# Modulation weights fetched one step ahead of their sums, and the last gate vector moved to the last stage's second product

## The chip, the cores and the metric

One Trainium2 chip, one of its NeuronCores. The metric is the device time of one execution in microseconds (us); each kernel has a median over several runs and one profiled execution, whose trace is what is read below. In the rows PE is TensorE (PEld its weight loads), DVE is VectorE, ACT is ScalarE, POOL is GpSimd and SP is SyncE, which here only issues DMAs. A "q" behind the name means the engine's sequencer.

## The reference, cut to what matters

A residual stream x of 512 rows by 1024 columns passes four stages: differential attention, a gated feed-forward product (FFN 1), a token mixer and a second feed-forward product (FFN 2), then a final norm. Stages two to four are modulated by a vector c of 1024 numbers:

```python
mod = (jax.nn.silu(c) @ ada_w[l] + ada_b[l]).reshape(B, N_SUBLAYERS, 3, D_MODEL)
shift, scale, gate = mod[:, :, 0], mod[:, :, 1], mod[:, :, 2]
...
h = modulate(rms_norm_2(x, norm_g[l, 2]), shift[:, 2], scale[:, 2])
x = x + 0.5 * gate[:, 2, None, :] * swiglu(h, ffn2_w_in[l], ffn2_w_out[l])
```

So there are nine modulation vectors of 1024, named (s, kind) below: stage s = 0, 1, 2 for FFN 1, mixer and FFN 2, kind = 0 shift, 1 scale, 2 gate. Each needs a 1024 x 1024 block of `ada_w`, 4 MB, to be read once. The gate (2, 2) is needed only when the second product of FFN 2 is added to x.

## The kernel before

Every large product is done in three TensorE passes: a float32 operand is split into a rounded high part and the rest (`split`, L105: ACT makes the high part, DVE the low part), and high x high, high x low and low x high are summed in PSUM. Weights come by the SP queue into three rotating `raw` buffers (L110) and are split into `whi` and `wlo`, four buffers each. Nearly all other SBUF tiles, the modulation's among them, are taken from one pool of 61 slots of 128 x 512 (`tile`, L102).

**Order.** TensorE's instructions run in the order in which the program emits them. Side work is put into that order by a clock of the program's own: each matmul adds its estimated time to `self.now` (L85), and `later(delay, fn)` (L67) queues a function that is called when the clock passes its due time. `run_until` (L76) calls queued functions early, moving the clock to their due times, until a condition holds. DVE, ACT, POOL and SP get their orders from a scheduler that places what is emitted by priority; each of these queues then runs in order.

**One modulation vector** (`ada`, L446) is made in two halves of 512 columns. For each half, eight steps `one(k, half, acc)` (L463) are queued `step` apart. Step k starts a 256 KB DMA of 128 rows of `ada_w` into a tile `araw` (L466) and right behind it emits the DVE instruction that multiplies it by one column of silu(c) and adds it to `acc` (L469 for k = 0, L471 for the others). After step 7 the sum is split (`ahi`, `alo`), and 21.24 program us later (`DL["ada"]`) `go` (L490) has TensorE sum it over the 128 rows: two products with a tile of ones, 512 columns each, whose result DVE adds to the bias and stores as the half of the vector (L494 to L499). Only one vector is in work at a time (`ada_next`, L504). With `scratch` the tiles lie in the buffers of `hT`, the transposed normed input, which are free between the two products of an FFN, and the fetches go by POOL's DMA queue with four places in rotation; without it they lie in the pool of slots and the fetches go by SP's queue, between the weights' own.

**Where the vectors are made.** (0, 0) and (0, 1) in attention with a step of 6 program us, (0, 2) late in attention with 3; (1, 0) and (1, 1) at the start of the second product of FFN 1, with `scratch`, 2.5; (1, 2), (2, 0) and (2, 1) one after the other in the mixer, 2.5; (2, 2) at the start of FFN 2, 3.0 (L895). `ada_wait` (L509) runs queued work until a vector is complete; `next_norm` (L941) calls it when the first row tile of a stage is finished.

**An FFN** (`ffn`, L874). The first product makes the hidden activations by column blocks of 256: the first block plainly (`gemm_quad`), the other ten by a seven-product Strassen scheme (`fast_feat`, L239), whose sums of weight quarters `S` (L232) and of results `u`, `d` (L266) are DVE's and POOL's work. The second product (`gemm_tok`, L137) splits the activations (`gs`) as it reaches them and multiplies them with `ffn_w_out`, in two halves of 512 columns, each 264 matmuls for four row tiles. When a row tile of a half is summed, `gated_add` (L410) multiplies it by the gate (L427), adds it to x and squares it for the next norm. FFN 1 and FFN 2 run the same code on the same shapes.

Of the kernel before, what the change touches and what calls it, by code (L numbers as in the profile page):

```python
# [18 lines left out]
D = 1024  # L19
KD = D // P  # L20
# [21 lines left out]
class Net:  # L42
# [367 lines left out]
    def gated_add(self, gate, squares, then=None):  # L410

        nc = self.nc

        def evict(half, t, bank):
            if half and then:
                with self.tc.high_priority(offset=PRIO):
                    finish(half, t, bank)
                    then(t)
            else:
                finish(half, t, bank)  # L420

        def finish(half, t, bank):
            if gate is None:
                nc.vector.tensor_tensor(self.x[t][half], bank, self.x[t][half], op=ALU.add)
            else:
                tmp = self.tile("tmp")
                nc.vector.tensor_tensor(tmp, bank, gate[half], op=ALU.mult)  # L427
                nc.vector.tensor_tensor(self.x[t][half], self.x[t][half], tmp, op=ALU.add)
            if squares:
                self.norm_half(t, half)  # L430

        return evict
# [13 lines left out]
    def ada(self, s, kind, step, scratch=False):  # L446


        nc, a = self.nc, self.a
        dst = self.mod[s, kind] = [None, None]  # L450
        if scratch:
            if self.scratch is None:
                self.scratch = [self.hp.tile([P, KD, S], dt, tag=f"hT{i}", name=f"ada{i}") for i, dt in ((0, F32), (1, F32R))]
                self.turn = {}
            sc = self.scratch

        def tile_(name, dt=F32, places=None):
            if not scratch:
                return self.tile(name, dt)
            n = self.turn[name] = self.turn.get(name, -1) + 1  # L460
            return sc[0 if dt == F32 else 1][:, places[n % len(places)], :]

        def one(k, half, acc):  # L463
            c0 = s * 3 * D + kind * D + half * 512
            raw = tile_("araw", places=(0, 1, 6, 7))
            (nc.gpsimd if scratch else nc.sync).dma_start(raw, a["ada_w_2"][0, k * P:(k + 1) * P, c0:c0 + 512])  # L466
            if k == 0:
                acc = tile_("aacc", places=(2, 3))
                nc.vector.tensor_scalar(acc, raw, self.silu_c[:, 0:1], None, op0=ALU.mult)  # L469
            else:  # L470
                nc.vector.scalar_tensor_tensor(acc, raw, self.silu_c[:, k:k + 1], acc, op0=ALU.mult, op1=ALU.add)  # L471
            if k < KD - 1:
                self.later(step, lambda: one(k + 1, half, acc))
                return
            ab = self.tile("ab")
            self.bcast(ab, a["ada_b_2"][0, c0:c0 + 512])
            gb = None
            if kind == 1:
                gb = tile_("gb", places=(4, 5))
                self.bcast(gb, a["norm_g_2"][0, s, half * 512:half * 512 + 512])  # L480
            hi, lo = tile_("ahi", F32R, (0, 1)), tile_("alo", F32R, (2, 3))
            self.split(hi, lo, acc)
            self.later(DL["ada"], lambda: go(half, hi, lo, ab, gb))
            if half == 0:
                self.later(step, lambda: one(0, 1, None))
            else:
                self.ada_busy = False
                self.later(step, self.ada_next)

        def go(half, hi, lo, ab, gb):  # L490
            b = self.bank("sc")
            self.mm(b, self.ones, hi, True, False)
            self.mm(b, self.ones, lo, False, True)
            nc.vector.tensor_tensor(ab, b, ab, op=ALU.add)  # L494
            if kind == 1:
                nc.vector.scalar_tensor_tensor(ab, ab, 1.0, gb, op0=ALU.add, op1=ALU.mult)
            if kind == 2 and s != 1:
                nc.vector.tensor_scalar(ab, ab, 0.5, None, op0=ALU.mult)
            dst[half] = ab  # L499

        self.ada_queue.append(lambda: one(0, 0, None))
        self.ada_next()

    def ada_next(self):  # L504
# [369 lines left out]
    def ffn(self, s, win, wout, nxt):  # L874
        nc = self.nc
        sg, gT, gs = {}, {}, {}

        def gate(i):
            def done(bank, d0, d1):
                for o, d in ((d0[:, :256], bank), (d1, d1), (d0[:, 256:], d0[:, 256:])):  # L880
                    nc.scalar.activation(o, d, AF.Silu)
                sg[i] = d0, d1
            return done

        def up(i):
            def done(bank, *d):
                c = slice(0, 256), slice(256, 512)
                nc.vector.tensor_tensor(d[0][:, c[0]], bank, sg[i][0][:, c[0]], op=ALU.mult)
                nc.gpsimd.tensor_tensor(d[1], d[1], sg[i][1], op=ALU.mult)
                nc.gpsimd.tensor_tensor(d[0][:, c[1]], d[0][:, c[1]], sg[i][0][:, c[1]], op=ALU.mult)  # L890
                for n in range(2):
                    gT[2 * i + n] = d[n]
            return done

        if s == 2:  # L895
            self.ada(2, 2, 3.0)
        wts = [self.load_w(win[g * 512:(g + 1) * 512, c0:c0 + 256], 4, 256) for c0 in (0, FFN) for g in range(2)]
        sta = lambda n: lambda k: tuple(x[:, k % 4, n % 2 * P:n % 2 * P + P] for x in wts[n // 2 * 2 + k // 4])
        first = [self.tile("d0") for _ in range(2)]
        sg[0] = first  # L900

        def ev_up(n, bank):
            gT[n] = sg[0][n]
            nc.vector.tensor_tensor(gT[n], bank, gT[n], op=ALU.mult)

        self.gemm_quad([sta(n) for n in range(4)],
                       [lambda b, n=n: nc.scalar.activation(first[n], b, AF.Silu) for n in range(2)] +
                       [lambda b, n=n: ev_up(n, b) for n in range(2)])
        def split_g(k):
            if k not in gs:  # L910
                gs[k] = self.tile("gs", F32R), self.tile("gs", F32R)
                self.split(*gs[k], gT[k])

        def act(k, t):
            split_g(k)
            return tuple(g[:, t * P:(t + 1) * P] for g in gs[k])

        self.fast_feat([(win[:, c0 + i * 256:c0 + i * 256 + 256], fn(i))
                        for i in range(1, FFN // 256) for c0, fn in ((0, gate), (FFN, up))],
                       lambda: [split_g(k) for k in range(DL["gs"])])  # L920
        if s == 0:
            self.ada(1, 0, 2.5, True)
            self.ada(1, 1, 2.5, True)

        self.ada_wait((s, 2))
        self.norm_reset()
        for half in range(2):
            ev = self.gated_add(self.mod[s, 2], True, self.lazily(nxt) if half else None)
            self.gemm_tok(act, KF, wout[:, half * 512:half * 512 + 512], lambda t, b: ev(half, t, b), 4 if half else 0)
# [512 lines left out]
```

## Time and profile before

| | |
|---|---|
| median of 3 runs | 1874.91 us (1872.62 to 1875.62) |
| the profiled execution | 1875.19 us, span of its instructions 1873.4 us |
| mean granted TensorE clock | 0.992 of full speed |
| busy: PE, PEld, DVE, ACT, POOL | 97%, 86%, 75%, 50%, 21% of the span |
| first product of FFN 1, of FFN 2 | from 597.80 to 831.24 us, from 1501.41 to 1742.55 us |
| fetches of `ada_w` | 112 by SP into `araw`, 32 by POOL into the scratch |

Times in rows are us from the start of the span. An idle time in a row stands in brackets with what ended it; a wait for several things is put down to the last of them.

### The profile page before, as it was taken

The page shows a single profiled execution, that of the slowest core. Times are in us where ns is not written, and L with a number is a line of the kernel's source. Part 1 is how long each engine was busy: PE and PEld are TensorE (multiplying, and loading weights), DVE is VectorE, ACT ScalarE, POOL GpSimd, SP SyncE. Part 2 cuts the span into 40 slices and gives each one's busy share as a digit, 9 for nine tenths or more (in the row PEclk, how much of TensorE's full clock was granted, in tenths as well). Part 3 has the DMA queues.
Part 4 walks back from the last instruction along what each step waited for, and adds up shares of the span by engine and source line. Part 5 has one row for each costly group of instructions (what it writes and reads, how often), then busy time and mean ns, then how long its engine had stood idle before and what let it go on. Part 6 is the DMA issues. An engine that isn't in the chain of part 4 may idle for free.

```text
span 1873.4 us, 29092 instructions
## 1 busy us (share of the span) xinstructions
PE 1820.4 (97%) x10799; PEld 1604.3 (86%) x10799; DVE 1407.5 (75%) x2904; ACT 932.4 (50%) x1696; POOL 400.2 (21%) x380
## 2 busy tenths in 40 slices
PE   8999999999999999999999999999999998999997
PEld 5888777788888999998898778888888898999886
DVE  5568677776966899998365788777868799999633
ACT  5577575465653454553235745664433344554521
POOL 3213114042012122332030211212110022232001
PEclk9999999999999999999999999999999999999999
DMA  4535533625422233357324322222347343333431
GB/s 165 140 113 147 146 107 116 205 67 147 138 92 75 69 106 110 102 173 255 106 69 119 85 57 63 63 62 77 108 157 234 113 135 125 113 102 102 124 113 56
DMA packets 187618, 217.93 MB, mean 116 GB/s; under 512 B 9618, under 2 KB 129826, under 8 KB 187476
## 3 DMA queue, kind: packets, MB, share of 16 engines
q1 hardware_dynamic: 181168, 196.88, 34.9%
q0 software_dynamic: 5584, 18.08, 3.1%
q8 instruction: 85, 1.39, 0.3%
q10 hardware_dynamic: 724, 1.12, 0.2%
q14 instruction: 57, 0.47, 0.1%
HBM read 201.34 MB, written 2.11 MB: 109 GB/s over the span
## 4 chain that ended last, share of the span: by engine, by line
PE 80%; DVE 10%; issue 4%; ACT 2%; POOL 2%; DMA 2%; SPq 0%; POOLq 0%; DVEq 0%; ACTq 0%
PE acc L84 69%; PE sc L84 5%; DVE wlo L107 2%; PE av L84 2%; PE sc L95 1%; DMA araw<-in_ada_w_dram 1%; DVE cvy L1039 1%; PE tr L95 1%; PE tr L785 1%; DVE S L232 1%; PE tr L84 1%; POOL rs L305 1%; ACT whi L106 1%; DMA raw<-in_ffn_w_out_dram 0%; POOL rqk L1094 0%
## 5 line engine op out<-in xcount | busy, mean ns | idle before, releaser
L84 PE MATMUL acc<-hT,whi 128*128 128x256 f32 (+1 forms) x2704 | 642.5, 331 | 5.3 <-DVE d L266 4.8
L84 PEld LDWEIGHTS acc<-hT,whi 128*128 128x128 f32 x2704 | 447.4, 192 | 38.8 <-DVE d L266 5.2
L107 DVE TENSOR_TENSOR wlo<-raw,whi 128x1024 fp32r<-128x1024 f32 (+1 forms) x325 | 331.1, 1028 | 164.3 <-ACT whi L106 162.1
L84 PE MATMUL acc<-hT,wlo 128*128 128x256 f32 (+1 forms) x1352 | 441.2, 326 | 2.9 <-DVE wlo L107 2.8
L106 ACT CAST whi<-raw 128x1024 fp32r<-128x1024 f32 (+1 forms) x325 | 285.5, 880 | 309.9 <-PE acc L84 249.0
L84 PEld LDWEIGHTS acc<-hT,wlo 128*128 128x128 f32 x1352 | 258.5, 191 | 26.1 <-DVE wlo L107 4.1
L84 PE MATMUL acc<-whi,hT 128*128 128x512 f32 x768 | 266.6, 404 | 1.9 <-DVE o L802 0.7
L84 PE MATMUL acc<-whi,gs 128*128 128x512 f32 x704 | 219.1, 390 | 1.8 <-DVE gs L107 1.8
L305 POOL TENSOR_TENSOR rs<-ms,mhalf 128x8 f32<-128x8 f32 (+2 forms) x60 | 86.3, 1439 | 448.9 <-DVE ms L303 360.5
L84 PE MATMUL acc<-T,whi 128*128 128x256 f32 x960 | 174.5, 283 | 0.0
L84 PEld LDWEIGHTS acc<-whi,hT 128*128 128x128 f32 x768 | 144.5, 189 | 32.1 <-DVE hT L107 2.3
L106 ACT CAST whi<-S 128x512 fp32r<-128x512 f32 x160 | 99.4, 621 | 118.7 <-DVE S L232 90.5
L84 PEld LDWEIGHTS acc<-whi,gs 128*128 128x128 f32 x704 | 132.0, 188 | 29.9 <-DVE gs L107 2.6
L84 PE MATMUL acc<-wlo,hT 128*128 128x512 f32 x384 | 150.9, 393 | 3.0 <-DVE wlo L574 3.0
L84 PEld LDWEIGHTS acc<-T,whi 128*128 128x128 f32 x960 | 149.7, 192 | 0.0
L107 DVE TENSOR_TENSOR wlo<-S,whi 128x512 fp32r<-128x512 f32 x160 | 138.6, 885 | 0.5 <-ACT whi L106 0.2
L84 PE MATMUL acc<-wlo,gs 128*128 128x512 f32 x352 | 137.0, 389 | 0.0
L84 PE MATMUL acc<-T,wlo 128*128 128x256 f32 x480 | 135.8, 283 | 0.0
L232 POOL TENSOR_TENSOR S<-raw,S 128x512 f32<-128x512 f32 x40 | 66.8, 1670 | 204.4 <-DVE S L232 196.0
L770 ACT ACTIVATE p<-p,mn 128x128 f32<-128x128 f32 (+3 forms) x128 | 71.1, 556 | 47.4 <-DVE mn L766 45.7
L84 PEld LDWEIGHTS acc<-T,wlo 128*128 128x128 f32 x480 | 92.2, 192 | 0.0
L471 DVE SCALAR_TENSOR_TENSOR aacc<-araw,silu_c,aacc 128x512 f32<-128x512 f32 x98 | 78.9, 805 | 14.0 <-DMA araw<-in_ada_w_dram 13.2
(299 smaller groups left out, 3106.1 us busy)
## 6 DMA issues: line engine op xcount, KB each, us to landing
raw<-in_ffn_w_in_dram SPq DMA_DIRECT2D x88, 512.0 KB, 3.6
raw<-in_l_w_in_dram SPq DMA_DIRECT2D x60, 512.0 KB, 4.1
araw<-in_ada_w_dram SPq DMA_DIRECT2D x112, 256.0 KB, 4.6
raw<-in_mix_w_in_dram SPq DMA_DIRECT2D x53, 512.0 KB, 3.8
raw<-in_ffn_w_out_dram SPq DMA_DIRECT2D x44, 512.0 KB, 3.8
raw<-in_l_w_out_dram SPq DMA_DIRECT2D x16, 512.0 KB, 3.7
ada<-in_ada_w_dram POOLq DMA_DIRECT2D x32, 256.0 KB, 4.2
ab<-in_ada_b_dram POOLq DMA_DIRECT2D x18, 256.0 KB, 4.0
```

The source lines that it names most:

```text
L84: self.nc.tensor.matmul(out, a, b, start=start, stop=stop, skip_group_check=onto)
L95: self.nc.tensor.transpose(out[:, j * P:(j + 1) * P], src(j), self.ident)
L106: return (self.nc.scalar.copy(hi, src), self.nc.vector.tensor_tensor(lo, src, hi.bitcast(F32), op=ALU.subtract))
L107: self.nc.vector.tensor_tensor(lo, src, hi.bitcast(F32), op=ALU.subtract))
L232: sub = lambda o, x, y, op=ALU.subtract, e=nc.vector: e.tensor_tensor(o, x, y, op=op)
L305: pin(nc.gpsimd.tensor_tensor(r[:, :n], ms[:, :n], self.mhalf[:, :n], op=ALU.pow))
L471: nc.vector.scalar_tensor_tensor(acc, raw, self.silu_c[:, k:k + 1], acc, op0=ALU.mult, op1=ALU.add)
L770: nc.scalar.activation(p_[m][:, :L], p_[m][:, :L], AF.Exp, bias=mn[:, m:m + 1], scale=-1.0, accum_out=st[:, m, b:b + 1])
L785: nc.tensor.transpose(tr[:, c * P:(c + 1) * P], p0[:, c * P:(c + 1) * P], self.ident)
L1039: nc.vector.scalar_tensor_tensor(y[:, j:], r[:, :S - j], cw[:, 3 - j, n:n + 1], y[:, j:], op0=ALU.mult, op1=ALU.add)
```

## The change

Three edits. (1) The fetch of step k + 1 is started in step k, ahead of step k's sum, and handed on; the first fetch of a vector is started by `begin`, and its first sum follows one `step` later. (2) The gate vector (2, 2) is no longer queued at the start of FFN 2 with a step of 3.0, by SP and in the pool of slots, but between the two products of FFN 2 with a step of 1.5, by POOL's queue and in the buffers of `hT`. (3) The wait for the gate ahead of the second product stays for FFN 1 only; in its place `finish` runs queued work until the half of the gate that it multiplies by is there.

```diff
@@ -420,6 +420,7 @@
         def finish(half, t, bank):
+            self.run_until(lambda: gate is None or gate[half] is not None)
             if gate is None:
@@ -460,17 +461,22 @@
-        def one(k, half, acc):
+        def fetch(k, half):
             c0 = s * 3 * D + kind * D + half * 512
             raw = tile_("araw", places=(0, 1, 6, 7))
             (nc.gpsimd if scratch else nc.sync).dma_start(raw, a["ada_w_2"][0, k * P:(k + 1) * P, c0:c0 + 512])
+            return raw
+
+        def one(k, half, acc, raw):
+            c0 = s * 3 * D + kind * D + half * 512
+            nxt = fetch((k + 1) % KD, half + (k + 1) // KD) if k < KD - 1 or half == 0 else None
             if k == 0:
                 acc = tile_("aacc", places=(2, 3))
                 nc.vector.tensor_scalar(acc, raw, self.silu_c[:, 0:1], None, op0=ALU.mult)
             else:
                 nc.vector.scalar_tensor_tensor(acc, raw, self.silu_c[:, k:k + 1], acc, op0=ALU.mult, op1=ALU.add)
             if k < KD - 1:
-                self.later(step, lambda: one(k + 1, half, acc))
+                self.later(step, lambda: one(k + 1, half, acc, nxt))
                 return
@@ -482,7 +488,7 @@
             if half == 0:
-                self.later(step, lambda: one(0, 1, None))
+                self.later(step, lambda: one(0, 1, None, nxt))
             else:
@@ -498,7 +504,11 @@
-        self.ada_queue.append(lambda: one(0, 0, None))
+        def begin():
+            raw = fetch(0, 0)
+            self.later(step, lambda: one(0, 0, None, raw))
+
+        self.ada_queue.append(begin)
         self.ada_next()
@@ -892,8 +902,6 @@
-        if s == 2:
-            self.ada(2, 2, 3.0)
         wts = [self.load_w(win[g * 512:(g + 1) * 512, c0:c0 + 256], 4, 256) for c0 in (0, FFN) for g in range(2)]
@@ -921,8 +929,9 @@
         if s == 0:
             self.ada(1, 0, 2.5, True)
             self.ada(1, 1, 2.5, True)
-
-        self.ada_wait((s, 2))
+            self.ada_wait((s, 2))
+        else:
+            self.ada(2, 2, 1.5, True)
         self.norm_reset()
```

## Rows read from the trace of the kernel before

**Rows 1.** The page: busy time and share of the span of each engine.

```profile
PE 1820.4 (97%) x10799; PEld 1604.3 (86%) x10799; DVE 1407.5 (75%) x2904; ACT 932.4 (50%) x1696; POOL 400.2 (21%) x380
```

**Rows 2.** Busy time by stretch: length, PE, PEld, DVE, ACT, POOL; clock, DMA share, GB/s.

```profile
597.80:831.24 233.44, 231.07 (x1921) 230.00 (x1920) 214.55 (x327) 114.70 (x219) 64.68 (x43) 1.00 0.33 104
1501.41:1742.55 241.14, 233.28 (x1925) 232.08 (x1924) 223.99 (x350) 116.17 (x221) 68.19 (x46) 0.99 0.37 118
831.24:890.00 58.76, 57.79 (x256) 47.48 (x255) 51.37 (x73) 23.46 (x34) 20.17 (x37) 1.00 0.81 263
1742.55:1801.50 58.95, 58.14 (x258) 47.81 (x257) 29.41 (x38) 22.25 (x32) 0.74 (x1) 1.00 0.33 105
```

**Rows 3.** Timeline of DVE, then of PE, around two stops in FFN 2.

```profile
1553.13 0.74 DVE L471 SCALAR_TENSOR_TENSOR aacc<-araw,silu_c,aacc 128x512 f32<-128x512 f32 x1
1553.79 0.68 DVE L266 TENSOR_TENSOR d<-u,acc 128x512 f32<-128x512 f32 x1
...
1554.52 0.50 PE L84 MATMUL acc<-hT,whi 128*128 128x256 f32 x2 [2.28 <-DVE d L266]
...
1567.84 0.80 PE L84 MATMUL acc<-hT,whi 128*128 128x256 f32 x2 [2.53 <-DVE d L266]
```

**Rows 4.** Busy time by stretch again, behind a stop in attention and one in FFN 2.

```profile
359.20:362.70 3.50, 3.50 (x10) 2.72 (x9) 2.60 (x9) 1.89 (x5) 0.00 (x0) 0.51 0.36 132
1567.60:1571.00 3.40, 3.16 (x15) 3.16 (x16) 2.87 (x6) 3.10 (x6) 1.15 (x1) 0.50 0.04 11
```

**Rows 5.** The instructions of tile `araw`: ns min/median/max; DVE idle until; issue to landing.

```profile
L471 DVE SCALAR_TENSOR_TENSOR aacc<-araw,silu_c,aacc x98: 726/746/1637, 125.0 to 1564.4; 128x512 f32<-128x512 f32 x98
...
  DMA araw<-in_ada_w_dram: 25.9, 22
...
DMA to landing us min/median/max: 2.6/4.6/7.5
```

**Rows 6.** Timeline of DVE and PE: two waits for `araw` in attention, PE behind them.

```profile
274.83 0.75 DVE L471 SCALAR_TENSOR_TENSOR aacc<-araw,silu_c,aacc 128x512 f32<-128x512 f32 x1 [1.62 <-DMA araw<-in_ada_w_dram]
...
279.29 0.41 PE L785 MATMUL tr<-ident,p 128*128 128x128 f32 x2 [2.26 <-DVE qkl L702]
...
309.24 0.49 DVE L469 TENSOR_SCALAR aacc<-araw,silu_c 128x512 f32<-128x512 f32 x1 [1.61 <-DMA araw<-in_ada_w_dram]
...
310.47 0.47 PE L84 MATMUL acc<-whi,hT 128*128 128x512 f32 x1 [0.73 <-DVE o L802]
```

**Rows 7.** Timeline of ACT and PE: ACT held by a sum's split, PE behind it, attention.

```profile
294.30 0.62 ACT L106 CAST ahi<-aacc 128x512 fp32r<-128x512 f32 x1 [3.27 <-DVE aacc L471]
...
295.67 0.63 PE L95 MATMUL tr<-ident,o 128*128 128x128 f32 x4 [1.62 <-ACT qraw L678]
...
357.80 0.62 ACT L106 CAST ahi<-aacc 128x512 fp32r<-128x512 f32 x1 [2.62 <-DVE aacc L471]
...
358.63 0.49 PE L84 MATMUL av<-v,wt 128*128 128x128 f32 x2 [2.16 <-ACT wt L788]
```

**Rows 8.** Timeline of PE and DVE: the last two sums over rows in the mixer.

```profile
1467.88 0.40 PE L84 MATMUL sc<-ahi,ones 128*128 128x512 f32 x1
...
1474.28 0.69 DVE L107 TENSOR_TENSOR alo<-aacc,ahi 128x512 fp32r<-128x512 f32 x1
...
1482.69 0.40 PE L84 MATMUL sc<-ahi,ones 128*128 128x512 f32 x1
```

**Rows 9.** The instructions of tile `ada`, FFN 1's scratch: ns min/median/max, first and last start.

```profile
L471 DVE SCALAR_TENSOR_TENSOR ada<-ada,silu_c x28: 732/747/753, 837.7 to 884.6; 128x512 f32<-128x512 f32 x28
...
L469 DVE TENSOR_SCALAR ada<-ada,silu_c x4: 482/524/909, 836.3 to 872.6; 128x512 f32<-128x512 f32 x4
...
DMA to landing us min/median/max: 2.9/4.2/6.5
```

**Rows 10.** Timeline: first ones-product in FFN 1's second product; first gate use in FFN 2.

```profile
873.99 0.64 PE L84 MATMUL sc<-ada,ones 128*128 128x512 f32 x2
...
1800.51 0.69 DVE L427 TENSOR_TENSOR tmp<-acc,ab 128x512 f32<-128x512 f32 x1
```

## The prediction

> **What bounds the kernel now.** I read the page's busy times first: TensorE is busy for 1820.4 of 1873.4 us [rows 1]. Only 53 us are left in which it stands still, so a change of this kind can win no more than the stops that it removes, and the clock that such stops cost. The second view is the busy time by stretch. FFN 1 and FFN 2 run the same code on the same shapes, which gives each first product a twin: 233.44 us for FFN 1, 241.14 us for FFN 2 [rows 2]. What FFN 2 has more is the gate vector (2, 2), made inside it. The third view is the timeline where TensorE stops there. At 1554.52 it had waited 2.28 us, at 1567.84 it had waited 2.53 us, both times for DVE's `d` (L266), which empties the PSUM bank that the next product wants; just ahead of that `d` DVE worked off sums of `araw`, one of them at 1553.13 [rows 3]. DVE is busy for 224 of the 241 us [rows 2], so what is put between its Strassen sums comes out as lateness. Behind the second stop the clock stands at 0.50 of full speed, its lower level of 1.2 GHz, for 3.4 us, as it does behind a stop in attention [rows 4].
>
> The fourth view is the tile `araw`: DVE stood idle for its fetches 22 times, 25.9 us in all [rows 5]. Most of that costs nothing: in the mixer the waits of TensorE list no stop from 1318 to 1501 us, where many of these idle times lie. In attention two of them stand directly ahead of a stop of TensorE [rows 6], and twice ACT was held at the head of its queue by the split of a sum, with what TensorE wanted (a PSUM copy, a transposed weight) queued behind it [rows 7].
>
> **The change, part by part.**
>
> *The gate leaves the first product of FFN 2.* Removed there: 16 fetches on SP's queue, which stood between weight loads; 16 sums on DVE at 0.746 us (0.484 for the two first ones) [rows 5, 9], 11.4 us in all, with two splits and the adds behind them; two pairs of products with ones. The twin gives the worth: 241.14 - 233.44 = 7.70 us. It closes with its parts: the stops 2.28 + 2.53 = 4.81, half of 3.4 us at the lower clock = 1.7, and two pairs of ones-products, 0.64 each [rows 10], 1.28: together 7.79. The ones-products only move to the second product, so 7.70 - 1.28 = **6.4 us** are gained. What would be late next in this product is what is late in the twin, and there nothing stops TensorE after the first blocks.
>
> *The gate enters the second product of FFN 2.* Added: the same sums on DVE, 16 fetches on POOL's queue, two pairs of ones-products (counted above). DVE is busy for 29.41 of the first 58.95 us there, POOL for 0.74. The twin carries twice as many sums in the same place, with DVE busy for 51.37 of 58.76 us and POOL for 20.17, and TensorE is busy for 57.79 [rows 2]: it doesn't stop but for the 0.8 to 1 us that both stages lose at their start. So the cost is 0; the cover is DVE's idle half. The fetches wait until TensorE has read the last of `hT`; the twin's first sum runs at 836.3, 5.1 us into its stage, and its 32 sums take until 885.4, 1.53 us each [rows 2, 9]. For FFN 2 this gives sums from 1747.6 to 1772. Where does TensorE want them? The program's clock runs at 1.104 us of the trace to one of its own here: FFN 1's first ones-product, due at 7 x 2.5 + 21.24 = 38.74, ran 42.75 us into the stage [rows 2, 10]. With `begin` and a step of 1.5 the two halves fall due at 33.24 and 45.24, that is at 1779 and 1792. The sums are done before both, and the first multiplication by the gate is at 1800.51 [rows 10]. The new wait in `finish` therefore finds its half made and calls nothing early. Queued on POOL behind the fetches are the broadcast of the final gain and the last norms, 50 us later or more.
>
> *Fetches one step ahead, attention.* Nothing is added on any engine; one more tile of the 61 slots is held per step, and SP issues a fetch one step earlier, ahead of one or two weight loads. At best every stop that I can tie to a sum goes: of the 2.26 us at 279.29 the 1.62 that DVE waited, the 0.73 at 310.47 [rows 6], the 1.62 at 295.67 and the 2.16 at 358.63 [rows 7], and 1.7 of clock behind the last [rows 4], 7.8 us. At worst DVE's, ACT's and SP's queues, which the scheduler orders anew, make one more stop like that at 358.63 with its clock, 3.9 us. I take what stands directly behind a wait for a fetch, 1.62 + 0.73 = **2.35 us** gained; the other two stops come from where a sum stands in DVE's order, and the fetch alone need not move it.
>
> *Fetches ahead, FFN 1 and mixer.* FFN 1's scratch has four places in rotation already, so POOL runs ahead of DVE with or without the edit: 0. In the mixer TensorE isn't stopped by sums: 0. But `begin` adds a step to each vector. In attention nobody wants them for long after. In the mixer three vectors in a row become 3 x 2.5 = 7.5 later by the program's clock, 8.3 us. The last ones-product there, that of (2, 1), is already called early: it comes 14.8 us behind the one before [rows 8] instead of 8 x 2.5 x 1.104 = 22.1, since the next norm wants the scale vector. It will stay at its place, while its sum comes later: its low part starts at 1474.28 and lasts 0.69, 7.7 us ahead of the product at 1482.69 [rows 8]. If all of the 8.3 us reaches it, TensorE waits 0.6; if DVE has been lagging, 0; with a weight split, a gate multiplication and an add on DVE ahead of it, some 3. I take **0.5 us** lost.
>
> *Sum.* 1875.19 - 6.4 - 2.35 + 0.5 = **1867 us**. The profiled execution, 1875.19, lies 0.3 us from the median of the runs, 1874.91, so the sum stands for the median too.
>
> **The rivals.**
>
> *A. The fetch ahead clears attention.* All the stops in rows 6 and 7 go, with the clock: 1875.2 - 6.4 - 7.8 = 1861. For it: ACT's two long holds, 3.27 and 2.62 us [rows 7], both end with a sum. Against: the sum at 357 us waited hardly at all for its fetch, its place in DVE's order did it.
>
> *B. Attention loses what FFN 2 wins.* The new order of its queues, one slot less and three weight loads behind an earlier fetch make stops of 4 us or somewhat more: 1875.2 - 6.4 + 3.9 + 0.5 = 1873, up to 1877. For it: the stops there come from queue heads that happen to be late, and a new order draws them anew. Against: DVE's and ACT's waits on a fetch can only get shorter.
>
> *C. The gate comes too late in the second product: slower.* TensorE's order has the ones-products at 1779 and 1792, and the sums have no other way to them; if the sums come slowly, TensorE stands still there with all of the second product queued behind. It decides from (1792 - 1747.6 - 1.3 for the split) / 16 = 2.7 us a step on. If each fetch waited for the sum before it, a step would be a landing, 4.2 us, and a sum, 0.75 [rows 9]: 16 x 4.95 = 79 us, the last at 1827, TensorE 36 us late, 1875 - 6.4 + 36 = 1905. Against: four places and the earlier fetch, and the twin's 1.53 us. On the move of these fetches from SP to POOL the rows show a landing of 4.2 us on POOL, in a stage where DVE is busy for 87% of the time, and 4.6 on SP [rows 2, 5, 9]. The Trainium skill's page "SBUF — State Buffer" (section "SBUF: two separate sides") speaks against the move: the descriptors of a DMA queued on GpSimd are written by GpSimd's cores, VectorE's two-port operations lock these out of the port that both share, and the transfer then waits. By that rule POOL's landings would be the longer ones and this rival the likely one; the trace, with the shorter landing on POOL, doesn't bear it out here.
>
> *D. FFN 2 keeps its stops.* DVE at 224 of 241 us might stop TensorE without the gate too, so that only small change is left: about 1875. Against: the twin has DVE at 214.55 of 233.44 us [rows 2], as dense, and no such stop.
>
> **How the numbers follow.** The forecast (1863 to 1871) gets 0.60, A 0.14, B 0.17, C 0.05, D 0.04. A measurement of this kernel can tell about 0.2% from no change, 3.7 us, so faster means below 1871.2. Faster: the forecast, A and a quarter of B, 0.78. Same: D and most of B, 0.15. Slower: C and the tail of B, 0.07. The range takes A at its lower end and B's 1873 with a little for the mixer's 3 us: 1860.5 to 1874; beyond lie the rest of B, C and part of D.
>
> **What would show it.** In the changed profile the first product of FFN 2 should take 233 to 235 us, without a wait of TensorE on `d` (L266) and with the clock at 1.00. In its second product the sums should run at 1.5 us spacing from 5 us into the stage, the ones-products without idle time ahead of them, DVE's share up. The idle time of DVE ahead of `araw` should fall from 25.9 us to a few. In the mixer the low part of the last sum should end within 1 us of its product. The prediction is wrong if stops of over 4 us new in sum appear in attention, if TensorE waits in front of a product with ones, or if the first product of FFN 2 stays above 238 us.

## The result, and the profile after

The changed kernel takes 1853.7 us (median, 1852.98 to 1856.94), 0.9896 of the kernel before (95% interval 0.9883 to 0.9908): 20.9 us less than the 1874.55 us of its four runs, where 8 were forecast, and below the range. The profiled execution has 1854.37 us and a span of 1852.6, 20.8 us shorter than the one before, so stage lengths of the two traces can be set against each other.

The page's busy times, as [rows 1]:

```profile
PE 1811.6 (98%) x10799; PEld 1598.0 (86%) x10799; DVE 1405.9 (76%) x2904; ACT 934.2 (50%) x1696; POOL 409.2 (22%) x396
```

TensorE lost more stops than the two that the gate made. Busy time by stretch (length, PE, PEld, DVE, ACT, POOL; clock, DMA share, GB/s) shows where. First attention of the kernel before, from the first score product to the last product with the output weights:

```profile
89.39:597.35 507.96, 494.56 (x2556) 416.06 (x2554) 363.41 (x796) 308.91 (x618) 115.70 (x94) 1.00 0.42 124
```

Then of the changed kernel the same stretch, FFN 2's first product, and the start of its second product:

```profile
88.11:584.82 496.71, 491.72 (x2556) 415.22 (x2554) 359.42 (x796) 309.98 (x618) 116.54 (x94) 1.00 0.43 126
...
1486.32:1719.37 233.05, 230.47 (x1922) 229.85 (x1920) 214.75 (x328) 116.12 (x220) 66.40 (x44) 1.00 0.33 102
1719.37:1778.32 58.95, 58.15 (x257) 47.68 (x256) 40.93 (x57) 22.84 (x33) 10.49 (x19) 1.00 0.58 185
```

Attention is 507.96 - 496.71 = 11.3 us shorter, FFN 2's first product 241.14 [rows 2] - 233.05 = 8.1 us. The second product is as gapless as before over its first 58.95 us, with DVE up from 29.41 us [rows 2] to 40.93. Over its whole length it is 1.1 us longer. The end behind the last matmul is 1.3 us longer, the start of the kernel 1.3 and the mixer 2.3 us shorter; the change leaves the start alone and the mixer nearly so, and both come back below.

Attention's part can be read off the waits of TensorE from 118 to 376 us (waiting line, what it waited for: us in all, times, longest). The kernel before:

```profile
PE av L84 <- ACT wt L788: 5.3, 3, 2.2
PE tr L785 <- DVE qkl L702: 2.3, 1, 2.3
PE tr L95 <- ACT qraw L678: 1.6, 1, 1.6
PE tr L785 <- DVE mn L766: 1.4, 1, 1.4
PE tr L95 <- POOL qraw L685: 1.0, 1, 1.0
PE sc L84 <- DVE qkl L702: 1.0, 1, 1.0
PE acc L84 <- DVE o L802: 0.7, 1, 0.7
```

The changed kernel:

```profile
PE av L84 <- ACT wt L798: 1.6, 1, 1.6
PE sc L84 <- DVE qkl L712: 1.5, 1, 1.5
PE tr L795 <- DVE qkl L712: 1.0, 1, 1.0
PE sc L84 <- DVE x L425: 0.9, 1, 0.9
```

13.3 us of waits became 5.0, and the stretch at the lower clock behind 358.63 [rows 4] is gone. Two of three waits for `wt`, ACT's copies of transposed attention weights, and the one for its PSUM copy `qraw` went. DVE's waits for fetches, by contrast, are nearly all there over the whole kernel. The instructions of tile `araw` in the changed kernel, as [rows 5]:

```profile
  DMA araw<-in_ada_w_dram: 23.3, 23
...
DMA to landing us min/median/max: 2.6/4.3/7.6
```

23.3 us against 25.9, though 16 fetches fewer are in it. In attention alone they fell from 10.8 to 6.6 us, in eight waits both times. So a fetch that is started a step earlier still lands too late about as often, and attention lost over half of its stops all the same. That was the open question.

### The profile page after: what moved, and what is told of

Read it like the earlier page. It is cut to its first block, busy times and chain, and to the rows that moved or that the text cites. A ratio compares the mean times of both kernels' runs of the same rounds, so it can differ in the third digit from the quotient of the medians.

```text
span 1852.6 us, 29069 instructions
## 1 busy us (share of the span) xinstructions
PE 1811.6 (98%) x10799; PEld 1598.0 (86%) x10799; DVE 1405.9 (76%) x2904; ACT 934.2 (50%) x1696; POOL 409.2 (22%) x396
## 5 line engine op out<-in xcount | busy, mean ns | idle before, releaser
L84 PEld LDWEIGHTS acc<-wlo,hT 128*128 128x128 f32 x384 | 72.5, 189 | 14.7 <-DVE wlo L584 3.7
```

The source lines that it names most:

```text
L84: self.nc.tensor.matmul(out, a, b, start=start, stop=stop, skip_group_check=onto)
```

## The experiments

Theory 1: sums no longer wait for fetches. Theory 2: the sums stand elsewhere in the orders of DVE and ACT, since `begin` moves them by a step. Theory 3, formed on the first results: ACT no longer stands at the head of its queue at the split of a finished sum. The runs in one table; each ratio is against runs of the kernel before on the same chip, whose medians lie between 1872.6 and 1876.0 us, so rows are compared by their ratios and traces rather than by their medians. "Attention" is the stretch above in us, "ACT" its idle time ahead of `ahi` and "DVE" that ahead of `araw` from 118 to 376 us.

| run | median us | ratio (95%) | attention | ACT | DVE |
|---|---|---|---|---|---|
| before | | 1 | 507.96 | 7.8 | 10.8 |
| changed | 1853.7 | 0.9896 (0.9883 to 0.9908) | 496.71 | 0.9 | 6.6 |
| gate_only | 1866.8 | 0.9971 (0.9960 to 0.9982) | 508.89 | 7.9 | 9.7 |
| ahead_only | 1857.37 | 0.9920 (0.9900 to 0.9940) | 495.93 | 0.9 | 6.3 |
| step_later | 1866.99 | 0.9972 (0.9961 to 0.9984) | 503.57 | 6.4 | 11.4 |
| ahead_no_delay | 1863.28 | 0.9951 (0.9935 to 0.9968) | 498.37 | 0 | 10.0 |
| split_later | 1861.0 | 0.9927 (0.9909 to 0.9946) | 496.65 | 1.7 | 12.0 |
| no_ada01 | 1855.62 | 0.9897 (0.9879 to 0.9915) | 489.76 | none | none |
| half_step | 1854.78 | 0.9895 (0.9877 to 0.9912) | 496.05 | 0 | 14.7 |
| gate_sync | 1852.85 | 0.9884 (0.9869 to 0.9899) | 496.19 | 0.9 | 7.1 |
| last_in_step | 1858.84 | 0.9934 (0.9916 to 0.9952) | 499.96 | 3.6 | 11.1 |
| only_last_ahead | 1864.38 | 0.9959 (0.9946 to 0.9972) | 499.93 | 0 | 11.7 |
| all_sync | 1850.49 | 0.9888 (0.9873 to 0.9903) | 495.94 | 0.9 | 5.8 |
| cut_sync | 1852.24 | 0.9900 (0.9885 to 0.9914) | 496.11 | 0 | 6.5 |

**The two halves of the change.** gate_only: the kernel before with the gate moved as in the change.

> The gate vector (2, 2) is moved to the second product of FFN 2, the fetches stay in the step of their sums. Both theories: FFN 2's first product takes its twin's 233 to 235 us instead of 241, the second product 1 us more for the two pairs of ones-products; attention is as before. 1867 to 1868 us, about 7 below the kernel before. If fetches in the step of their sums make the gate late, TensorE waits ahead of its ones-products and the time is above 1870.

ahead_only: the changed kernel with the gate put back.

```diff
+        if s == 2:
+            self.ada(2, 2, 3.0)
         wts = [self.load_w(win[g * 512:(g + 1) * 512, c0:c0 + 256], 4, 256) for c0 in (0, FFN) for g in range(2)]
...
-            self.ada_wait((s, 2))
-        else:
-            self.ada(2, 2, 1.5, True)
+        self.ada_wait((s, 2))
```

> The fetches one step ahead, the gate vector (2, 2) left at the start of FFN 2. Both theories: the whole gain of the changed kernel outside FFN 2, that is attention 11 us shorter than before (the trace of the changed kernel against the one before), 1861 to 1863 us. If the two edits need each other, it is above 1866.

gate_only came out as expected, ahead_only some 4 us below what was expected. The two ratios multiply to 0.9891, the whole change within its interval: the halves don't need each other. In gate_only attention is as before and FFN 2's first product takes 233.29 us; here are that stretch and the start of the second product:

```profile
1502.07:1735.36 233.29, 230.39 (x1922) 229.78 (x1920) 213.87 (x328) 115.32 (x219) 66.23 (x45) 1.00 0.34 103
1735.36:1794.30 58.94, 58.33 (x255) 47.87 (x256) 41.70 (x59) 23.50 (x34) 10.35 (x19) 1.00 0.56 181
```

In ahead_only that first product keeps the gate and still takes 237.62 us, 3.5 less than before: TensorE's waits for `d` there fall from 4.8 to 2.4 us, and its clock doesn't drop. So the earlier fetch alone takes away part of what the move of the gate takes away there.

**Earlier fetch or later sum.** step_later (an edit of the kernel before) moves sums and fetches together, ahead_no_delay (an edit of ahead_only) has the fetches ahead without the shift of the sums:

```diff
-        self.ada_queue.append(lambda: one(0, 0, None))
+        self.ada_queue.append(lambda: self.later(step, lambda: one(0, 0, None)))
```

> Neither edit: only the first sum of each vector one step later, its fetch with it, so that all the sums stand where the changed kernel has them while each fetch stays in the step of its sum. Theory 1 (the fetch ahead is what helps: sums no longer wait for fetches): nothing gained, 1872 to 1877 us, attention's stops 13 us as before. Theory 2 (what helps is that sums and splits stand one step later between attention's heads, in other places of DVE's and ACT's orders): attention some 10 us shorter, 1862 to 1866 us.

```diff
-            self.later(step, lambda: one(0, 0, None, raw))
+            one(0, 0, None, raw)
```

> The fetches one step ahead, but the sums at the due times of the kernel before (no step added by begin), the gate at its old place. Theory 1 (the fetch ahead helps): attention some 10 us shorter, 1861 to 1866 us, DVE's idle time ahead of araw well below 25.9 us. Theory 2 (the sums' places help): the sums stand where they stood, 1872 to 1877 us.

Neither theory held as it stood. The shift alone won 4.4 us in attention, where theory 2 asked some 10. The earlier fetch alone won 9.6, as theory 1 asked, but not by its mechanism: DVE's waits for fetches stayed at 10.0 us in the window and 23.7 in the whole kernel, against 10.8 and 25.9. The column that follows attention's length is another one. In the kernel before, gate_only and step_later ACT stands for 6 us or more ahead of `ahi` and attention takes 503 us and up; in the changed kernel, ahead_only and ahead_no_delay it stands for less than 1 us and attention takes 500 and below. The kernel before shows what that means. Timeline of ACT at the third of the four splits:

```profile
289.66 1.37 ACT L699 ACTIVATE qkT<-tr,cols 64x512 fp32r<-64x512 f32 x2
294.30 0.62 ACT L106 CAST ahi<-aacc 128x512 fp32r<-128x512 f32 x1 [3.27 <-DVE aacc L471]
294.94 0.59 ACT L678 COPY qraw<-acc 128x512 f32<-128x512 f32 x1
```

ACT has work to do; but at the head of its queue stands the split, whose sum isn't finished, and the PSUM copy `qraw` runs right behind it. TensorE stopped for `qraw` at 295.67 [rows 7].

**The split by itself.** split_later, an edit of the kernel before, leaves fetches and sums at their old due times and emits only the split a step later:

```diff
-            hi, lo = tile_("ahi", F32R, (0, 1)), tile_("alo", F32R, (2, 3))
-            self.split(hi, lo, acc)
-            self.later(DL["ada"], lambda: go(half, hi, lo, ab, gb))
+            def cut(rest=DL["ada"]):
+                hi, lo = tile_("ahi", F32R, (0, 1)), tile_("alo", F32R, (2, 3))
+                self.split(hi, lo, acc)
+                self.later(rest, lambda: go(half, hi, lo, ab, gb))
+
+            if s == 0 and kind < 2:
+                self.later(step, lambda: cut(DL["ada"] - step))
+            else:
+                cut()
```

> The kernel before with one thing moved: in attention's vectors (0, 0) and (0, 1) the split of a finished half sum is emitted one step (6 program us) behind its last sum, the products with ones at their old due times; fetches, sums and the gate (2, 2) as before. Theory 3 (what the fetch ahead removes is ACT standing at the head of its queue at the split, with PSUM copies and transposed weights behind it): the 7.8 us that ACT stands there between 118 and 376 us fall below 2, TensorE's stops near 234, 294 and 357 go (5.4 us, and a stretch at the lower clock), 1865 to 1868 us. If the holds only accompany stops that have another cause: 1870 to 1875 us, stops in attention 11 to 14 us.

It gave 11.3 us in attention, as much as the changed kernel, with DVE waiting 12.0 us for fetches and ACT's holds down from 7.8 to 1.7 us. Its time is some 4 us below the expected range. TensorE's waits from 118 to 376 us in split_later:

```profile
PE tr L791 <- DVE qkl L708: 2.6, 1, 2.6
PE av L84 <- ACT wt L794: 1.6, 1, 1.6
PE sc L84 <- DVE qkl L708: 1.0, 1, 1.0
```

The stop that ended at 279.29 before, which the prediction tied to a fetch [rows 6], is still there, at 2.6 us; those behind ACT are gone but one, and with them the smaller ones for `mn`, `o` and POOL's `qraw`.

ACT's hold is not all of it. The split has two instructions, ACT's high and DVE's low part, and split_later moves both. The stop for `mn` comes ahead of ACT's first hold (228.02); there DVE's low part `alo` of the first split stands right ahead of the instruction that makes `mn`. Timeline of DVE and PE, first the kernel before, then split_later, where the two have changed places and the stop is gone:

```profile
172.24 0.68 DVE L107 TENSOR_TENSOR alo<-aacc,ahi 128x512 fp32r<-128x512 f32 x1
172.95 0.29 DVE L766 CUSTOM_DVE_ANT_0 p<-sc,bias 128x128 f32<-128x128 f32 x1
...
173.39 0.63 PE L785 MATMUL tr<-ident,p 128*128 128x128 f32 x4 [1.43 <-DVE mn L766]
```

```profile
170.09 0.29 DVE L772 CUSTOM_DVE_ANT_0 p<-sc,bias 128x128 f32<-128x128 f32 x1
...
174.77 0.68 DVE L107 TENSOR_TENSOR alo<-aacc,ahi 128x512 fp32r<-128x512 f32 x1
```

What the run shows is that the place of the split costs the 11.3 us; no run moves its two halves one by one. Nor does a hold cost anything by itself: in the mixer of the kernel before, from 1318 to 1501 us, ACT stands as long for the same reason, and TensorE has no stop there. ACT's waits in that stretch:

```profile
ACT ahi L106 <- DVE aacc L471: 7.2, 3, 3.6
```

**The floor.** no_ada01, an edit of the kernel before, leaves out the fetches, sums and products of the vectors (0, 0) and (0, 1) and puts bias and norm gain in their place:

```diff
+            if s == 0 and kind < 2:
+                for half in range(2):
...
+                    self.bcast(ab, a["ada_b_2"][0, c0:c0 + 512])
...
+                    dst[half] = ab
...
+                return
```

> The kernel before without the fetches, sums and products of the vectors (0, 0) and (0, 1): in their place stand bias and norm gain alone, so a part of the computation is left out. It gives the floor of attention without that work. If the sums are behind nearly all of attention's stops (13.4 us from 118 to 376 us), these fall to 3 us or less, and attention with the fetches ahead (5 us of stops) has nearly nothing left to win: 1855 to 1859 us. If the heads themselves make the stops, more than 6 us of them stay: above 1862 us.

One wait is left from 118 to 376 us:

```profile
PE sc L84 <- DVE qkl L715: 1.0, 1, 1.0
```

So this work was behind nearly all of the stops in that window. Work of 28 us on DVE, which is busy for 363 of attention's 508 us, cost 18 us of length, some 2 of them TensorE's products with ones themselves; 11 the change gets back.

**Is it a lucky place?** half_step puts the changed kernel's sums half a step earlier (`step / 2` in `begin`), with the fetches still a step ahead.

> The changed kernel with the first sum of each vector half a step behind the first fetch instead of a whole one, so that all sums shift by 3 program us in attention while the fetches stay one step ahead. If the fetch ahead makes the gain, it doesn't depend on the shift: ACT's holds at the splits stay below 1.5 us and attention's stops at 4 to 6 us, 1852 to 1856 us. If the gain is a lucky place of the sums: attention's stops somewhere between 4 and 11 us, 1856 to 1861 us.

The fetch ahead holds up without the shift's full step: attention 496.05 us, ACT's holds 0, though DVE waits longer for fetches than in any other run, 14.7 us. cut_sync adds the later split to the changed kernel (and SP's fetches for the gate, below):

> The changed kernel with the gate's fetches on SP's queue (as in gate_sync) and, in attention, the split one step behind the last sum (as in split_later). With the fetches ahead ACT hardly stands at the splits any more (0.94 us), so by theory 3 the later split adds nothing: attention as in the changed kernel within 1 us, 1851 to 1854 us, as gate_sync. If split and fetch each remove stops of their own, attention gets 3 to 6 us shorter, towards the 489.8 us of the kernel without these sums: below 1850 us.

0.6 us in attention: with the fetch ahead there is hardly a hold left for a later split to take away.

**Which of the eight fetches.** only_last_ahead (an edit of the kernel before, of which the main lines are shown) starts only the last fetch of each half early, last_in_step (an edit of the changed kernel) all but the last:

```diff
+            if raw is None:
+                raw = fetch(k, half)
+            nxt = fetch(k + 1, half) if k == KD - 2 else None
```

> The kernel before with the last fetch of each half alone (k = 7) one step ahead; seven fetches stay in the step of their sums, the gate (2, 2) at its old place. Theory 3: nearly the whole gain of the fetches ahead, ACT's holds below 1.5 us, attention's stops at 4 to 6 us, 1859 to 1864 us. If the gain is spread over all sums: 1870 to 1876 us.

```diff
-            nxt = fetch((k + 1) % KD, half + (k + 1) // KD) if k < KD - 1 or half == 0 else None
+            if raw is None:
+                raw = fetch(k, half)
+            nxt = fetch((k + 1) % KD, half + (k + 1) // KD) if k != KD - 2 and (k < KD - 1 or half == 0) else None
```

> The changed kernel with the last fetch of each half (k = 7) back in the step of its sum; the other seven stay one step ahead. Theory 3 (ACT's hold at the split is what costs, and the split stands behind the last sum alone): the holds come back to 5 to 8 us, attention loses 7 to 11 us of the gain, 1860 to 1865 us. If the gain is spread over all sums: an eighth of it is lost, 1853 to 1857 us.

The last fetch alone wins 8.0 of ahead_only's 12.0 us in attention; its time is 0.4 us above the range that theory 3 gave. Taking it away brings back holds of 3.6 us and costs 3.3 us in attention, less than theory 3 asked on both counts; the time lies between the two expected ranges. By length the two runs are equal, with holds of 0 and of 3.6 us. Part of that is the clock: behind its stop near 276 us only_last_ahead has 3.4 us at half clock, the lower of the two levels, which costs some 1.7 us, and last_in_step has none in attention. Busy time by stretch in only_last_ahead:

```profile
276.40:279.80 3.40, 3.40 (x10) 2.65 (x9) 3.35 (x10) 1.70 (x4) 3.11 (x3) 0.51 0.91 289
```

TensorE's idle time in attention (length less PE's busy time) leaves the clock out: 13.4, 8.8, 7.5 and 6.4 us in the kernel before, step_later, last_in_step and only_last_ahead, with holds of 7.8, 6.4, 3.6 and 0 us. The order is that of the holds, the size isn't. The other seven fetches and the shift thus do part of it by another way, which no run here takes apart.

**The end of the kernel.** gate_sync and all_sync change the queue that the scratch fetches use:

```diff
-            (nc.gpsimd if scratch else nc.sync).dma_start(raw, a["ada_w_2"][0, k * P:(k + 1) * P, c0:c0 + 512])
+            (nc.gpsimd if scratch and s < 2 else nc.sync).dma_start(raw, a["ada_w_2"][0, k * P:(k + 1) * P, c0:c0 + 512])
```

(all_sync: `nc.sync` always.)

> The changed kernel with the 16 fetches of the gate vector (2, 2) on SP's queue instead of POOL's, still in the buffers of the transposed input between the products. POOL's last drain took 6.64 us with 73 DMAs issued by POOL and 7.95 us with 89, 0.082 us for each. If it counts POOL's DMAs: 6.6 us again, the end 1.3 us earlier, 1852 to 1853 us by the median against 1853.7. If SP stands at a scratch place with weight loads queued behind it, TensorE stops in the second product and it is above 1856 us.

> The changed kernel with all fetches of modulation weights on SP's queue, those of the scratch too: 41 DMAs are left to POOL instead of 89. By 0.68 us and 0.082 for each, its last drain takes 4.0 us instead of 7.95, and the end is then set by the landing of the last stores: 3.5 us earlier, 1850 to 1851 us. If SP stands at scratch places in FFN 1's second product, where POOL stood 24 us for DVE, with weight loads queued behind, TensorE stops there by more than 3 us and it is at 1854 us or above.

The longest of POOL's drains at the program's end (ns min/median/max), first the kernel before, then the changed one:

```profile
L1438 POOLq DRAIN  x3: 40/102/6639, 1866.0 to 1873.1; - x3
```

```profile
L1447 POOLq DRAIN  x3: 40/93/7946, 1843.9 to 1852.3; - x3
```

POOL issued 73 DMAs in the first and 89 in the second. gate_sync, with 73, has 6637 ns, and all_sync, with 41:

```profile
L1447 POOLq DRAIN  x3: 40/93/4024, 1843.3 to 1848.2; - x3
```

The 4.0 us that were expected for all_sync came out. SP's fetches hold up no weight load: TensorE is busy for 57.98 of the 58.78 us at the start of FFN 1's second product. From the start of the last matmul the program takes 7.9 us to its end in all_sync, 10.3 in gate_sync and 11.6 in the changed kernel. The runs' times don't separate these three: the intervals of their ratios overlap, and the kernel before took 1872.64 us beside all_sync, the fastest by its median, against 1874.55 beside the changed kernel.

## Why the prediction was wrong

The step that failed is "Fetches one step ahead, attention", forecast at 2.35 us with 7.8 as its best case; ahead_only shows 12.0 in its trace. It failed in two places.

First, it took the small stops and left the large ones. What stood behind DVE's waits for a fetch [rows 6] did shrink as forecast, the stop at 279.29 from 2.26 to 1.0 us and the one at 310.47 to nothing, though DVE's waits did not fall to a few us as it said. But it left what stood behind ACT [rows 7], because "the fetch alone need not move it". It did move: the last fetch alone, started early, ends ACT's holds (only_last_ahead), and a later split takes 6.1 of their 7.8 us without any early fetch and wins 11.3 us, with the stop of 279.29 still in place (split_later). DVE's waits for fetches, 12.0 us in that run and 14.7 in half_step, are longer than before and leave attention as short as in the changed kernel; a split that stands too early puts everything that follows in the queues of ACT and DVE behind it, and that the prediction had put at nothing.

Second, its best case was too small. It counted the stops that stood next to a fetch or a hold in the timeline. It left out the one for `mn` (1.43 us, behind DVE's half of the split), the one for `wt` at 235.35 (1.59 us, 7 us behind ACT's hold at 228.02) and POOL's `qraw` at 323.09 (0.99 us), which are gone in split_later as in the changed kernel. That a hold makes later work late fits the last two but is argued, not shown one by one. no_ada01, which leaves 1.0 us of stops, is the bound that should have been looked for: 12.3 of the 13.3 us were open to the edit.

Not all of the 20.8 us between the two traces need be the change's. The start has 1.3 us more in the kernel before, in code where nothing changed, and the mixer 2.3 us, with its stops nearly the same (8.5 and 8.8 us). What the traces show to differ in both is the clock. Busy time by stretch, the kernel before:

```profile
14.50:18.00 3.50, 3.50 (x13) 2.78 (x12) 0.30 (x1) 0.56 (x1) 0.00 (x0) 0.51 1.05 404
1069.20:1076.00 6.80, 6.55 (x24) 5.84 (x25) 3.73 (x8) 4.01 (x9) 1.91 (x3) 0.50 0.28 78
1086.30:1089.70 3.40, 3.40 (x10) 2.63 (x9) 3.30 (x13) 1.14 (x3) 0.00 (x0) 0.50 0.55 154
1110.20:1113.60 3.40, 3.40 (x15) 3.13 (x14) 3.40 (x29) 0.67 (x2) 0.00 (x0) 0.50 0.00 0
```

The changed kernel has none in its start and two in its mixer:

```profile
1058.40:1061.80 3.40, 3.40 (x11) 2.81 (x12) 1.84 (x4) 2.02 (x4) 1.44 (x1) 0.50 0.56 154
1072.00:1075.40 3.40, 3.40 (x13) 2.92 (x13) 3.40 (x12) 0.46 (x1) 0.00 (x0) 0.51 0.52 141
```

The mixer moves without the edit, too: 498.87 us in gate_only, there by longer stops, and 496.67 in split_later, both with its old emission. The stages that the edits touch hold 17.0 of the 20.8 us (11.3 + 8.1 - 1.1 - 1.3); by the medians of ahead_only and gate_only against the kernel before on their chip the two edits are worth about 15 and 6 us.

The rest by its steps. *The gate out of the first product*: forecast 7.70, measured 8.1 (7.9 in gate_only); right for this change, and the twin was the right view: 233.05 us, no wait for `d`, clock at 1.00. *The gate into the second product*: forecast 1.28 for its products with ones, measured 1.1, no stop. Its sums ran as foreseen, its products later (forecast 37 and 50 us into the stage, measured 40 and 57), still ahead of the first gated add at 1778.48. The instructions of tile `ada` in that stage of the changed kernel (ns min/median/max, first and last start), then TensorE's timeline:

```profile
L477 DVE SCALAR_TENSOR_TENSOR ada<-ada,silu_c x14: 736/748/753, 1725.7 to 1747.4; 128x512 f32<-128x512 f32 x14
```

```profile
1759.29 0.64 PE L84 MATMUL sc<-ada,ones 128*128 128x512 f32 x2
...
1776.14 0.64 PE L84 MATMUL sc<-ada,ones 128*128 128x512 f32 x2
```

*The end*: forecast nothing, measured 1.3 us; the step counted what was queued behind POOL's fetches and missed the drain at the program's end. *The mixer's late sum*: forecast 0.5 lost, measured 0. Its low part still ends 7.1 us ahead of its product, against 7.7 before, so that of the 8.3 us by which its emission moved only 0.7 came through, the case that the step priced at 0. Timeline of DVE and PE of the changed kernel:

```profile
1459.87 0.68 DVE L107 TENSOR_TENSOR alo<-aacc,ahi 128x512 fp32r<-128x512 f32 x1
...
1467.61 0.40 PE L84 MATMUL sc<-ahi,ones 128*128 128x512 f32 x1
```

Of the rivals, A was nearest in kind and 7 us short; C did not come: POOL's landings stayed at 4.2 us in the changed kernel with 48 of them, and the same 48 fetches by SP took 4.2 us in all_sync. The prediction held against the move what the Trainium skill's page "SBUF — State Buffer" (section "SBUF: two separate sides") says of VectorE's two-port operations. These landings show no delay, but they don't test the rule: no run here shows which of VectorE's operations are of that kind.

## What to carry to other kernels

When several engines run in order, look for the instruction that stands at the head of a queue waiting for side work, or just ahead of what the bottleneck wants, and count all that is queued behind it, not only the stop next to it; it costs something only where the bottleneck soon needs what is behind it. The remedy may be to emit that one instruction later, in attention here as good as fetching everything earlier. To bound such an edit, find the length of the stage without the side work (a twin in the trace, or a run without it) rather than add up the stops that look tied to it.

## What was not expected of the hardware

The drain of POOL's queue at the end of the program grows with the number of DMAs that POOL issued during the whole program, also with those that landed long before: 4.02 us with 41, 6.64 with 73 (in two kernels), 7.95 with 89. Each 256 KB fetch more on POOL's queue adds 0.082 us; whether it is the number, the bytes or the packets that count is not shown, since all the DMAs that were moved are alike. With SP's queue in their place the program's end behind the last matmul is 3.6 us shorter; the drain then ends at 1847.4 us, and SP's drains behind the landing of the last stores, which start at 1847.6, set the end.
